# A two-layer f32 model on one core: values of two heads in one product, x and z two pairs ahead, and a residual round behind one more projection

## The chip, the cores and the metric

The kernel runs on one core of a Trainium2 chip. The metric is the device time of one execution in microseconds, taken as the median of several executions. The profile is of one further execution of the same program.

## The reference, cut to what matters

The model has two layers, each with a feed-forward block behind it, on 512 tokens of width 1024. The first layer, the one that the change touches, joins an SSD mixer (16 heads of width 64, in two groups that share B and C) and a gated linear attention, GLA (4 heads, keys of 128, values of 256):

```python
proj = h @ w_in
z, xbc, dt_raw, q, k, v, g, gk_low = jnp.split(proj, ...)
xbc = silu(causal_depthwise_conv(xbc, conv_w, conv_b))      # x, B, C
dt  = softplus(dt_raw + dt_bias);  a_cum = cumsum(dt * -exp(a_log))
cb  = einsum(cm, bm)                                        # per chunk of 128
y_diag = einsum(cb, decay, x * dt)
states = einsum(bm, to_end, x * dt)                         # carried over the chunks
y_off  = einsum(cm, prev, exp(a_cum))
y = rms_norm_by_group((y_diag + y_off + x * d_skip) * silu(z))
# GLA: gk = log_sigmoid(gk_low @ gk_w2 + gk_b) / 16, scores and states in chunks of 64, times v
x = x + concatenate([y_ssd, y_gla]) @ w_out
x = x + swiglu(rms_norm(x))
```

The second layer is multi-head latent attention (MLA), followed by another feed-forward block. All of it is in f32.

## The kernel before, in words

**Products.** Activations lie transposed: eight tiles of 128 features by 512 tokens. TensorE (PE) multiplies in the type fp32r, so each f32 operand is split into a high part (ScalarE, ACT, casts it) and a low part (VectorE, DVE, subtracts). A product of two such operands is three matmuls, hi·hi, lo·hi and hi·lo (`mm3`, L172 to L174); eight such triples give one 128x512 tile (`dense`). A weight tile goes from a DMA on SyncE's queue into `wraw` (two buffers), then into `whi` on ACT (L164) and `wlo` on DVE (L165), three buffers each. These weights are issued with a priority that puts them ahead of what stands near them in the program. A buffer is free again when the last matmul that reads it is done.

**Banks.** Large products take turns on three PSUM banks called `acc`. Further banks are used by name: `st` for small sums, `a1`, `a2` (two) and `xt`.

**Start.** PE first runs eight matmuls on zeros (L101). The input x arrives tile by tile, is split, and the first product (`dtgk`: time steps and the gate's low-rank input) follows it. The second product is B of the first group. The sum of squares gives R, the reciprocal norm of each token, which scales every product when it is read from its bank.

**Pairs.** The 16 SSD heads are worked as eight pairs. For each pair f there is x (`conv`: product, scale by R, four taps L422 and L425, a tanh gate), z (`z_gate`, L293 to L297), and then:

- `core_in`: a DMA spreads the cumulated decays over partitions (`acb`); ACT makes the decay matrix `mt` (L476, L478), which DVE multiplies by cb (L480); PE turns x token-major (L488); DVE makes `xdt` (L492) and `xde` (L496).
- `core_states`: three matmuls (L505), then `hs`: one ACT copy (L509) and four DVE steps (L512) that carry the state.
- `core_out`: outputs from states (L525, made to wait for the last step of `hs`), outputs from within the chunk (L533), and four DVE steps to `y` (L537 to L540).

PE's waits for these small steps are hidden by large products put between them: each group of small matmuls is ordered behind a chosen matmul of a large product. `finish` squares y, and behind the pairs 3 and 7 a group norm over four y (L207 to L224, L547) gives the parts (`mxh`, `mxl`, L140 and L141) of four tiles of the mixer's output.

Before, x and z of pair 2 were made between pair 0's inputs and outputs, the values of GLA's head 0 covered pair 1, and from there x and z of pair f+1 covered pair f. The values' products (`values`, one head at a time) were 128x256.

**Behind the pairs.** `values(2)` and `values(3)` stand behind pair 7. Then GLA starts: the small weight `gk_w2` is split into `gw` (L639 to L642) and multiplied (L648). `project(h)` makes q and k of a head from two large products (DVE reads them from their banks as `qd`, L679, and `kr`). `out_round(r)` multiplies four tiles of mixer output by w_out and adds the result to x; round 0 covers pair 7, round 1 stands behind `project(0)`, and `project(1)` behind that.

The order of each engine's instructions comes from a scheduler that walks the program with priorities; `order(i, j)` adds that i stands behind j.

Of the kernel before, what the change touches and what calls it, by code (L numbers as in the profile page):

```python
# [8 lines left out]
F32 = mybir.dt.float32  # L9
# [9 lines left out]
P = 128  # L19
# [27 lines left out]
def kernel(ctx: ExitStack, tc: tile.TileContext, A, yT, stop=99):  # L47
# [52 lines left out]
    for j in range(8):  # L100
        E.matmul(ps, idle[:, 0:P], idle, start=True, stop=True)  # L101
# [42 lines left out]
    hold = []  # L144
# [6 lines left out]
    def weight_now(src, kc, m, home):  # L151
        raw = wp.tile([P, KD * P], F32, tag="wraw", name=nm("wraw"), bufs=2)
        r = raw[:, :kc * m]
        nc.sync.dma_start(r.rearrange("p (k m) -> p k m", k=kc), src)
        return parts(r, kc, m, home)

    def parts(r, kc, m, home=None):
# [6 lines left out]
        S.copy(hi[:, :kc * m], r)  # L164
        i = V.tensor_tensor(lo[:, :kc * m], r, hi.bitcast(F32)[:, :kc * m], ALU.subtract)  # L165
        if hold:
            order(i, hold[0], "weights that can wait behind a chain that cannot")
        return (hi[:, :kc * m].rearrange("p (k m) -> p k m", k=kc),
# [58 lines left out]
    def rstd_log(ssq, n, pool, tag):  # L227
# [10 lines left out]
        S.activation(R, R, AF.Exp, scale=-0.5)  # L238
# [7 lines left out]
    class Norm:  # L246
# [18 lines left out]
        def square(self, c, behind=None, pool=res, bufs=2):  # L265
# [5 lines left out]
            if self.ssq is None:  # L271
                self.ssq = sq
            else:
                V.tensor_tensor(sq, self.ssq, sq, ALU.add)
                self.ssq = sq
# [14 lines left out]
    def gate(pool, tag, ps, R, bufs):  # L290

        h = pool.tile([P, T], F32, tag="cva", name=nm(tag + "h"), bufs=2)
        V.scalar_tensor_tensor(h, ps, 0.5, R, ALU.mult, ALU.mult)  # L293
# [10 lines left out]
    for c in range(KD):  # L304
        nrm.add(c, later=True)
    with tc.tile_pool(name="sq0", bufs=4) as sq0:
        for c in range(KD):
            nrm.square(c, nrm.last, sq0, 4)
# [26 lines left out]
    with tc.tile_pool(name="gkp", bufs=1) as gkp:  # L335

        ps = aux("a1")
        dense(ps[:48], w_dtgk, xp)
# [13 lines left out]
        def steps(behind):  # L352
# [28 lines left out]
            S.activation(av, alog, AF.Exp)  # L381
# [24 lines left out]
        with tc.tile_pool(name="ssd", bufs=2) as sp:  # L406
# [4 lines left out]
            mm, zmm = {}, {"states": []}  # L411

            def conv(i, tag, bufs, bank=acc):

                w = weight(A["w_xbc"][i], KD, P)
# [6 lines left out]
                S.activation(a, xpad[:, 3:], AF.Identity, bias=cw[:, 48 + i:49 + i],  # L422
                             scale=cw[:, 36 + i:37 + i])
                for k in range(3):
                    V.scalar_tensor_tensor(a, xpad[:, k:k + T], cw[:, 12 * k + i:12 * k + i + 1], a,  # L425
                                           ALU.mult, ALU.add)
# [29 lines left out]
            def z_gate(f):  # L456
# [3 lines left out]
                return gate(sp, "z", ps, R, 2)  # L460

            def core_in(f, xs, cb, behind=None):

                acb = sp.tile([P, 2, T], F32, tag="acb", name=nm("acb"))
# [4 lines left out]
                S.activation(te, te, AF.Exp)  # L469
                cd = sp.tile([P, 2, 2], F32, tag="cd", name=nm("cd"))  # L470
                S.activation(cd, last[:, 1:3, :], AF.Exp)

                mt = sp.tile([P, 2, 4, P], F32, tag="mt", name=nm("mt"))
                for h in range(2):
                    for c in range(4):
                        S.activation(mt[:, h, c, :], acb[:, h, c * P:(c + 1) * P], AF.Relu, scale=-1.0,  # L476
                                     bias=act[:, c, 2 * f + h:2 * f + h + 1])
# [5 lines left out]
                for h in range(2):  # L483
                    S.activation(ea[64 * h:64 * h + 64, :], acb[64 * h:64 * h + 64, h, P:], AF.Exp)

                ps = aux("xt")
                for c in range(4):
                    i = E.transpose(ps[:, c * P:(c + 1) * P], xs[:, c * P:(c + 1) * P], ident)  # L488
                    if behind is not None:
                        order(i, behind, "x token-major in one go with the outputs of the heads before")  # L490
                xdt = sp.tile([P, 4, 2, 64], F32, tag="xdt", name=nm("xdt"))
# [6 lines left out]
                return f, xs, mt, ea, cd, xdt, xde  # L498

            def core_states(part, btok, behind):  # L500

                f, xs, mt, ea, cd, xdt, xde = part
                pst = aux("a2")
                for c in range(3):
                    i = E.matmul(pst[:, c * P:(c + 1) * P], btok[:, c, :],  # L505
                                 xde[:, c].rearrange("p h e -> p (h e)"), start=True, stop=True)
                    order(i, behind, "states behind products that run until x is ready")
                hs = sp.tile([P, 3, P], F32, tag="hs", name=nm("hs"), bufs=1)
                S.copy(hs[:, 0, :], pst[:, 0:P])  # L509
# [7 lines left out]
                return hs, ready  # L517

            def core_out(part, state, zg, cT, behind):

                hs, ready = state
                f, xs, mt, ea, cd, xdt, xde = part
                po = aux("a2")
                for c in range(3):
                    i = E.matmul(po[:, c * P:(c + 1) * P], hs[:, c, :], cT[:, (c + 1) * P:(c + 2) * P],  # L525
                                 start=True, stop=True)
                    order(i, behind, "outputs behind products that run until the states are ready")
                    wait_for(i, ready, "outputs in one go")
# [24 lines left out]
            def values(h):  # L553

                mms = []
                wv = [weight(A["w_v"][h, j], 4, 256) for j in range(2)]
                v = gkp.tile([P, 4, 256], F32, name=f"v{h}")
                for i in range(4):
                    ps = acc()
                    for k in range(KD):  # L560
                        wh, wl = wv[k // 4]
                        xh, xl = xp[k]
                        mms.append(mm3(ps[:, :256], xh[:, i * P:(i + 1) * P], xl[:, i * P:(i + 1) * P],
                                       wh[:, k % 4, :], wl[:, k % 4, :], k == 0, k == KD - 1))
                    S.activation(v[:, i, :], ps[:, :256], AF.Copy, scale=rtok[:, i:i + 1])
                vt[h] = v
                return mms

            rounds, ys, sums_sq = [], [], []

# [32 lines left out]
            part = core_in(2, xs[2], cb, end)  # L603
# [766 lines left out]
```

## Time and profile before

| | |
|---|---|
| median of three runs | 1343.99 us (1343.94 to 1344.37) |
| the profiled execution | 1347.43 us |
| its span, first to last instruction | 1345.2 us |
| busy in the span: PE / DVE / ACT | 1333.2 / 813.8 / 566.4 us |
| matmuls of PE | 6506 |
| mean granted clock of PE | 0.997 |
| first layer's mixer, by PE's timeline | about 0 to 408 us |

The profile names a group of instructions by its line in the kernel, the engine, the operation, and what it writes from what. "Idle before" is the time for which the engine stood still ahead of an instruction, and the name behind the arrow is the instruction that the profile takes for the releaser. Matmuls overlap, so a matmul's own duration is longer than the step from one start to the next. The granted clock is the share of full speed at which PE was let run in that stretch.

### The profile page before, as it was taken

The page shows a single profiled execution, that of the slowest core. Times are in us where ns is not written, and L with a number is a line of the kernel's source. Part 1 is how long each engine was busy: PE and PEld are TensorE (multiplying, and loading weights), DVE is VectorE, ACT ScalarE, POOL GpSimd, SP SyncE. Part 2 cuts the span into 40 slices and gives each one's busy share as a digit, 9 for nine tenths or more (in the row PEclk, how much of TensorE's full clock was granted, in tenths as well). Part 3 has the DMA queues.
Part 4 walks back from the last instruction along what each step waited for, and adds up shares of the span by engine and source line. Part 5 has one row for each costly group of instructions (what it writes and reads, how often), then busy time and mean ns, then how long its engine had stood idle before and what let it go on. Part 6 is the DMA issues. An engine that isn't in the chain of part 4 may idle for free.

```text
span 1345.2 us, 16692 instructions
## 1 busy us (share of the span) xinstructions
PE 1333.2 (99%) x6506; PEld 1094.7 (81%) x6506; DVE 813.8 (60%) x1387; ACT 566.4 (42%) x958; POOL 7.8 (1%) x35
## 2 busy tenths in 40 slices
PE   9999999999999999999999999999999999999998
PEld 6788889888888888888888887777788888888887
DVE  7878977778977444444333368987674444443221
ACT  7575634534344222233223338986543322222111
POOL 0000000000000000000000000000000000000000
PEclk9999999999999999999999999999999999999999
DMA  5333232322233323333333321100123323333331
GB/s 180 127 110 111 79 94 82 95 64 78 70 103 94 95 94 101 103 94 95 93 91 102 100 78 56 66 32 32 56 92 104 95 94 95 100 103 94 114 107 62
DMA packets 36782, 122.23 MB, mean 91 GB/s; under 512 B 4768, under 2 KB 5792, under 8 KB 36704
## 3 DMA queue, kind: packets, MB, share of 16 engines
q1 hardware_dynamic: 35888, 120.72, 28.8%
q8 instruction: 51, 0.84, 0.3%
q10 hardware_dynamic: 816, 0.46, 0.1%
q14 instruction: 27, 0.22, 0.1%
HBM read 119.03 MB, written 2.13 MB: 90 GB/s over the span
## 4 chain that ended last, share of the span: by engine, by line
PE 88%; DVE 5%; ACT 4%; DMA 1%; issue 1%; POOL 0%; SPq 0%; ACTq 0%; POOLq 0%; DVEq 0%
PE acc L172 26%; PE acc L173 26%; PE acc L174 26%; PE sco L1114 2%; PE po L1161 1%; PE ptr L1142 1%; DVE wlo L165 1%; ACT whi L164 1%; PE a L533 1%; ACT mt L476 1%; PE a L757 1%; DVE cva L425 0%; PE a L525 0%; PE a L762 0%; ACT xh L259 0%
## 5 line engine op out<-in xcount | busy, mean ns | idle before, releaser
L164 ACT CAST whi<-wraw 128x1024 fp32r<-128x1024 f32 (+1 forms) x218 | 224.7, 1031 | 558.6 <-PE acc L173 421.3
L172 PE MATMUL acc<-xh,whi 128*128 128x512 f32 x1144 | 449.7, 393 | 0.2 <-ACT qT L1089 0.2
L173 PE MATMUL acc<-xl,whi 128*128 128x512 f32 x1144 | 446.0, 390 | 0.0
L174 PE MATMUL acc<-xh,wlo 128*128 128x512 f32 x1144 | 445.8, 390 | 0.0
L165 DVE TENSOR_TENSOR wlo<-wraw,whi 128x1024 fp32r<-128x1024 f32 (+1 forms) x218 | 260.6, 1195 | 150.2 <-ACT whi L164 149.7
L172 PEld LDWEIGHTS acc<-xh,whi 128*128 128x128 f32 x1144 | 214.9, 188 | 45.2 <-issue 0.8
L174 PEld LDWEIGHTS acc<-xh,wlo 128*128 128x128 f32 x1144 | 214.8, 188 | 44.7
L173 PEld LDWEIGHTS acc<-xl,whi 128*128 128x128 f32 x1144 | 214.9, 188 | 44.1 <-issue 0.4
L827 DVE TENSOR_TENSOR fu<-acc,R 128x512 f32<-128x512 f32 x44 | 30.4, 691 | 137.6 <-PE acc L174 137.6
L174 PE MATMUL acc<-fhh,wlo 128*128 128x512 f32 x288 | 112.0, 389 | 0.0
L172 PE MATMUL acc<-fhh,whi 128*128 128x512 f32 x288 | 112.0, 389 | 0.0
L173 PE MATMUL acc<-fhl,whi 128*128 128x512 f32 x288 | 112.0, 389 | 0.0
L824 DVE TENSOR_TENSOR fg<-acc,R 128x512 f32<-128x512 f32 x44 | 30.4, 691 | 89.3 <-PE acc L174 89.3
L172 PEld LDWEIGHTS acc<-fhh,whi 128*128 128x128 f32 x288 | 54.1, 188 | 11.3
L174 PEld LDWEIGHTS acc<-fhh,wlo 128*128 128x128 f32 x288 | 54.1, 188 | 11.2
L173 PEld LDWEIGHTS acc<-fhl,whi 128*128 128x128 f32 x288 | 54.1, 188 | 11.2
L172 PE MATMUL acc<-mxh,whi 128*128 128x512 f32 x128 | 49.9, 392 | 0.0
L173 PE MATMUL acc<-mxl,whi 128*128 128x512 f32 x128 | 49.7, 389 | 0.0
L174 PE MATMUL acc<-mxh,wlo 128*128 128x512 f32 x128 | 49.7, 389 | 0.0
L1127 ACT ACTIVATE sc<-sc,mx 128x128 f32<-128x128 f32 (+3 forms) x64 | 35.9, 565 | 12.3 <-DVE mx L1125 12.1
L1114 PE MATMUL sco<-kT,qT 96*128 96x256 f32 (+3 forms) x128 | 39.5, 440 | 0.8 <-ACT qT L1089 0.5
L841 DVE TENSOR_TENSOR x<-x,acc 128x512 f32<-128x512 f32 x16 | 11.0, 688 | 42.9 <-PE acc L174 42.9
(363 smaller groups left out, 1608.2 us busy)
## 6 DMA issues: line engine op xcount, KB each, us to landing
wraw<-in_w_gate_dram SPq DMA_DIRECT2D x44, 512.0 KB, 3.5
wraw<-in_w_up_dram SPq DMA_DIRECT2D x44, 512.0 KB, 3.5
wraw<-in_w_down_dram SPq DMA_DIRECT2D x32, 512.0 KB, 3.5
wraw<-in_w_out_dram SPq DMA_DIRECT2D x16, 512.0 KB, 3.5
wraw<-in_w_xbc_dram SPq DMA_DIRECT2D x12, 512.0 KB, 3.6
wraw<-in_w_down_dram SPq DMA_DIRECT2D x16, 384.0 KB, 3.1
wraw<-in_w_z_dram SPq DMA_DIRECT2D x8, 512.0 KB, 3.6
wraw<-in_w_v_dram SPq DMA_DIRECT2D x8, 512.0 KB, 3.6
```

Of the source, the lines that this page charges most:

```text
L164: S.copy(hi[:, :kc * m], r)
L165: i = V.tensor_tensor(lo[:, :kc * m], r, hi.bitcast(F32)[:, :kc * m], ALU.subtract)
L172: E.matmul(out, ah, bh, start=first, stop=False)
L173: E.matmul(out, ah, bl, start=False, stop=False)
L174: return E.matmul(out, al, bh, start=False, stop=last)
L476: S.activation(mt[:, h, c, :], acb[:, h, c * P:(c + 1) * P], AF.Relu, scale=-1.0, bias=act[:, c, 2 * f + h:2 * f + h + 1])
L533: i = E.matmul(pd[64 * h:64 * h + 64, c * P:(c + 1) * P], xdt[:, c, h, :], mt[:, h, c, :], start=True, stop=True)
L757: i = E.matmul(po[e][:, r * P:(r + 1) * P], v[:, r, e * P:(e + 1) * P], sc[:, r, :], start=True, stop=(r == 0))
L824: V.tensor_tensor(g, pg, R, ALU.mult)
L827: V.tensor_tensor(u, pu, R, ALU.mult)
L1114: i = E.matmul(ps[:, at:at + n], self.qts[j][:, b * P:(b + 1) * P], self.kts[j][:, :n], start=True, stop=True)
L1127: S.activation(sc[:, at:at + n], sc[:, at:at + n], AF.Exp, bias=mx[:, j:j + 1], scale=-1.0, accum_out=sm[:, j:j + 1])
```

## The change

In the order of the program:

1. **Start.** Ten matmuls on zeros instead of eight. The first product takes each triple in the order hi·xh, lo·xh, hi·xl. The second product's weights are loaded and split in two halves, ahead of the squares, and the other weights' DMAs are ordered behind them. One exponential (`av`) is put behind the one of R.
2. **Values.** `values(h)` makes heads h and h+1 side by side as 128x512 products on four banks, with eight halves of weights loaded per tile pair. `values(0)` stands behind pair 3, `values(2)` covers pair 7.
3. **Pairs.** Before pair 1's states stand x and z of pair 3, and so on: x and z are made two pairs ahead (z has three buffers). `out_round(0)` covers pair 6. New orders put the rest of a covering product behind the states, and decays, first taps and z halves behind the states ahead of them.
4. **Residual round.** `project(1)` stands ahead of `out_round(1)`.
5. **Smaller.** The copies into `gw` have a high priority. Weights with a `home` (MLA's) are loaded through a tile of their own (`wrb`) and not through `wraw`.

```diff
-    for j in range(8):
+    for j in range(10):
         E.matmul(ps, idle[:, 0:P], idle, start=True, stop=True)
...
-        raw = wp.tile([P, KD * P], F32, tag="wraw", name=nm("wraw"), bufs=2)
+        if home is None:
+            raw = wp.tile([P, KD * P], F32, tag="wraw", name=nm("wraw"), bufs=2)
+        else:
+            raw = const.tile([P, T], F32, tag="rsb", name=nm("wrb"))
...
+    raw = wp.tile([P, KD * P], F32, tag="wraw", name="wraw_b", bufs=2)
+    w_b = [wp.tile([P, KD * P], F32R, tag=t, name=t + "_b") for t in ("whi", "wlo")]
+    b_split = []
+    for j in range(2):
+        at = slice(j * T, j * T + T)
+        first_in.append(nc.sync.dma_start(raw[:, at].rearrange("p (k m) -> p k m", k=4),
+                                          A["w_xbc"][8][:, 4 * j:4 * j + 4]))
+        b_split.append((S.copy(w_b[0][:, at], raw[:, at]),
+                        V.tensor_tensor(w_b[1][:, at], raw[:, at], w_b[0].bitcast(F32)[:, at], ALU.subtract)))
...
-        dense(ps[:48], w_dtgk, xp)
+        for k, (xh, xl) in enumerate(xp):
+
+            E.matmul(ps[:48], w_dtgk[0][:, k, :], xh, start=(k == 0), stop=False)
+            E.matmul(ps[:48], w_dtgk[1][:, k, :], xh, start=False, stop=False)
+            E.matmul(ps[:48], w_dtgk[0][:, k, :], xl, start=False, stop=(k == KD - 1))
...
-            S.activation(av, alog, AF.Exp)
+            order(S.activation(av, alog, AF.Exp), rstd_log.last, "one change of table for both")
...
-                return gate(sp, "z", ps, R, 2)
+                z = gate(sp, "z", ps, R, 3)
...
-                wv = [weight(A["w_v"][h, j], 4, 256) for j in range(2)]
-                v = gkp.tile([P, 4, 256], F32, name=f"v{h}")
+                vt[h], vt[h + 1] = (gkp.tile([P, 4, 256], F32, name=f"v{h + e}") for e in range(2))
+                banks = [acc() for _ in range(3)] + [aux("a1")]
+                for q in range(4):
+                    raw = wp.tile([P, KD * P], F32, tag="wraw", name=nm("wraw"), bufs=2)
+                    with tc.high_priority(offset=AHEAD):
+                        for e in range(2):
+                            nc.sync.dma_start(raw.rearrange("p (k e m) -> p k e m", k=2, e=2)[:, :, e, :],
+                                              A["w_v"][h + e, q // 2, :, 2 * (q % 2):2 * (q % 2) + 2])
+                        wh, wl = parts(raw, 2, T)
+                    for i in range(4):
+                        for k in range(2):
+                            xh, xl = xp[2 * q + k]
+                            mms.append(mm3(banks[i], xh[:, i * P:(i + 1) * P], xl[:, i * P:(i + 1) * P],
+                                           wh[:, k, :], wl[:, k, :], (q, k) == (0, 0), (q, k) == (3, 1)))
...
-            hs = core_states(part, btok, zmm[2][3])
-            y, end = core_out(part, hs, zg[0], cT, zmm[2][7])
-            part = core_in(1, xs[1], cb, end)
+            hs = core_states(part, btok, zmm[2][1])
+
+            order(zmm[2][3], hs[3], "the rest of the product behind the states")
+            for i in (part[7][-2], part[7][-1], conv_ops["in", 2]):
+                order(i, hs[2], "what can wait behind the states")
+            for i in (conv_ops[2], z_ops[2]):
+                order(i, hs[1], "the next pair's behind the states")
+            y, end = core_out(part, hs, zg[0], cT, zmm[2][-1])
+            outs = list(out_ops)
+            part = core_in(1, xs[1], cb, end, hs[2])
             finish(0, y)
-            rtok = tok_scalar(R)
-            v = values(0)
-            hs = core_states(part, btok, v[5])
-            y, end = core_out(part, hs, zg[1], cT, v[27])
...
+            for f in range(1, 8):
...
+                if f < 6:
+                    xs[f + 2] = conv(f + 2, "xs", 3)
+                    fill = mm[f + 2]
+                elif f == 6:
+                    fill = out_round(0, rounds[0])
                 else:
-                    mms = out_round(0, rounds[0])
-                    hs = core_states(part, btok, mms[3])
-                    last = mms[11]
+                    fill = values(2)
...
             q0, _ = project(0)
+            q1, last = project(1)
             out_round(1, rounds[1])
-            q1, last = project(1)
```

**What it moves on the engines, first place: DVE between the first pair's outputs and the second pair's states.** The rows are DVE's list before, from the carried states of pair 0 (`hs_112`) to the operand of pair 1's states (`xde_123`). `cva` and `xs` belong to x, `zh` and `z` to z, `y_115` to pair 0's output.

```order
L512 SCALAR_TENSOR_TENSOR hs_112_665<-hs_112_665,cd_90_555,a2_111_661 128x64 x4
L480 TENSOR_TENSOR mt_119_696<-mt_119_696,cb_76_489 128x512 x2
L538 TENSOR_TENSOR ea_92_569<-a2_113_671,ea_92_569 128x384
L165 TENSOR_TENSOR wlo_153_911<-wraw_151_908,whi_152_910 128x1024
L537 SCALAR_TENSOR_TENSOR y_115_684<-xs_58_375,pv_87,a2_114_675 128x512
L492 TENSOR_TENSOR xdt_122_716<-xt_121_711,dt_398 128x512
L539 TENSOR_TENSOR y_115_684<-y_115_684,ea_92_569 128x384
L496 TENSOR_TENSOR xde_123_718<-xdt_122_716,te_117_691 128x384
```

After the change the same stretch of DVE's list ends in these rows. Ahead of them, behind the four steps of pair 0's `hs`, stand two `cva` taps, `zh` and a third `cva` tap.

```order
L499 TENSOR_TENSOR te_143_837<-acb_142_835,act_553 128x6
L576 TENSOR_TENSOR ea_89_574<-a2_110_676,ea_89_574 128x384
L458 SCALAR_TENSOR_TENSOR xs_100_627<-cvt_99_625,cva_98_620 128x512
L307 SCALAR_TENSOR_TENSOR z_107_664<-zt_106_662,zh_105_660 128x512
L575 SCALAR_TENSOR_TENSOR y_112_689<-xs_55_380,pv_87,a2_111_680 128x512
L511 TENSOR_TENSOR mt_116_701<-mt_116_701,cb_73_494 128x512
L577 TENSOR_TENSOR y_112_689<-y_112_689,ea_89_574 128x384
L511 TENSOR_TENSOR mt_116_701<-mt_116_701,cb_73_494 128x512
L578 TENSOR_TENSOR y_112_689<-y_112_689,z_63_444 128x512
L527 TENSOR_TENSOR xdt_119_721<-xt_118_716,dt_403 128x512
L171 TENSOR_TENSOR wlo_153_872<-wraw_151_869,whi_152_871 128x1024
L531 TENSOR_TENSOR xde_120_723<-xdt_119_721,te_114_696 128x384
```

So `xde` of pair 1 now has the taps, z and x of pair 2 and all of y ahead of it, where before it had `mt`, two steps of y and a weight split. On PE, the states that read it stand 26 large matmuls behind the transposes (L522).

**Second place: PE at the second head's projections.** The rows are PE's list after the change, from the last triple of q1 into k1. `acc_412` is q1's bank, `acc_419` k1's; three banks back, `acc_395` is q0's. The names in brackets are engines for which the instruction waits.

```order
L180 MATMUL acc_412_2264<-xh_19_157,whi_410_2260 128x512
L181 MATMUL acc_412_2264<-xl_20_158,whi_410_2260 128x512
L182 MATMUL acc_412_2264<-xh_19_157,wlo_411_2261 128x512
L180 MATMUL acc_419_2303<-xh_5_129,whi_417_2299 128x512 [waits DVE_49,Activation_49]
L181 MATMUL acc_419_2303<-xl_6_130,whi_417_2299 128x512
L182 MATMUL acc_419_2303<-xh_5_129,wlo_418_2300 128x512
L709 MATMUL st_387_2145<-gx_245,gw_2132 128x512 [waits DMAHW3_49,DMAHW4_49,DMAHW1_49,DMAHW5_49,DMAHW0_49,DMAHW6_49,DVE_49,Activation_49]
```

Before, residual round 1 stood here, and the first product behind the values was q0, 24 matmuls later k0.

**Third place: DVE ahead of that matmul.** DVE's list after the change, from the last scalings of the group norm to the reads of the banks of q0, k0 and q1. `mxl` are the low parts of the mixer's output, `wlo_432` the low parts of residual round 1's second weights.

```order
L585 SCALAR_TENSOR_TENSOR y_342_1878<-y_342_1878,pv_87,Rg_378_2094 128x512
L141 TENSOR_TENSOR mxl_380_2107<-y_279_1539,mxh_379_2106 128x512
L141 TENSOR_TENSOR mxl_382_2112<-y_308_1680,mxh_381_2111 128x512
L141 TENSOR_TENSOR mxl_384_2117<-y_342_1878,mxh_383_2116 128x512
L585 SCALAR_TENSOR_TENSOR y_372_2078<-y_372_2078,pv_87,Rg_378_2094 128x512
L171 TENSOR_TENSOR wlo_432_2378<-wraw_430_2375,whi_431_2377 128x1024
L141 TENSOR_TENSOR mxl_386_2122<-y_372_2078,mxh_385_2121 128x512
L740 SCALAR_TENSOR_TENSOR qd_397_2204<-acc_395_2177,R_32_203 128x512
L753 TENSOR_TENSOR kr_403_2241<-acc_402_2216,R_32_203 128x512
```

Before, DVE's list at the reads of q0 and k0 was this:

```order
L650 TENSOR_SCALAR gm_2331<-st_398_2332,pv_87 128x512
L650 TENSOR_SCALAR gm_2331<-st_399_2336,pv_87 128x512
L679 SCALAR_TENSOR_TENSOR qd_408_2391<-acc_406_2364,R_32_192 128x512
L165 TENSOR_TENSOR wlo_426_2478<-wraw_424_2475,whi_425_2477 128x1024
L650 TENSOR_SCALAR gm_2331<-st_400_2340,pv_87 128x512
L650 TENSOR_SCALAR gm_2331<-st_401_2344,pv_87 128x512
L692 TENSOR_TENSOR kr_414_2428<-acc_413_2403,R_32_192 128x512
```

The weight parts rotate over three buffers (`wlo` in the order q0, k0, q1, k1, then the round's first and second weights), so `wlo_432` takes the buffer that q1's `wlo_411` held.

More of the change, by code (lines that the diff above doesn't have):

```diff
@@ L167, in parts @@
             order(i, hold[0], "weights that can wait behind a chain that cannot")
+        if len(hold) > 1:
+            order(cast, hold[1], "weights that can wait behind a chain that cannot")
         return (hi[:, :kc * m].rearrange("p (k m) -> p k m", k=kc),
@@ L273, in square @@
             else:
-                V.tensor_tensor(sq, self.ssq, sq, ALU.add)
+                i = V.tensor_tensor(sq, self.ssq, sq, ALU.add)
+                if behind_sum is not None:
+                    order(i, behind_sum, "sums of squares behind the first weights")
                 self.ssq = sq
@@ L483, in core_in @@
                 for h in range(2):
-                    S.activation(ea[64 * h:64 * h + 64, :], acb[64 * h:64 * h + 64, h, P:], AF.Exp)
+                    act_ops.append(S.activation(ea[64 * h:64 * h + 64, :], acb[64 * h:64 * h + 64, h, P:], AF.Exp))
+                if behind_act is not None:
+                    for i in act_ops:
+                        order(i, behind_act, "decays behind the states of the heads before")
                 ps = aux("xt")
@@ L516, in core_states @@
                                                ALU.mult, ALU.add)
-                return hs, ready
+                return hs, ready, first, last
             def core_out(part, state, zg, cT, behind):
-                hs, ready = state
-                f, xs, mt, ea, cd, xdt, xde = part
+                hs, ready = state[:2]
+                f, xs, mt, ea, cd, xdt, xde = part[:7]
                 po = aux("a2")
+                out_ops.clear()
                 for c in range(3):
@@ new lines @@
+            for f in range(1, 8):
+                cT_out = cT
+                if f == 3:
+                    bc = group(1)
+                if f < 6:
[3 more added lines that the diff above has]
+                    fill = out_round(0, rounds[0])
+                else:
+                    fill = values(2)
+                if f == 1:
+                    for i in outs:
+                        order(i, fill[1], "first outputs behind products that run until the decays are ready")
+                    order(fill[3], part[8], "the rest of the products behind x token-major")
+                hs = core_states(part, btok, fill[5 if f == 1 else 4])
+                if f == 3:
+                    cb, cT, btok = spread(*bc, fill[-1])
+                if f < 6:
+                    zg[f + 2] = z_gate(f + 2)
+                    last = zmm[f + 2][-1]
+                else:
+                    order(fill[6], hs[3], "the rest of the products behind the states")
+                    last = fill[11]
@@ L622 @@
                     part = core_in(f + 1, xs[f + 1], cb, end)
+                if f > 5:
+                    order(fill[13], part[8] if f < 7 else end, "the rest of the products behind the outputs")
                 finish(f, y)
-                if f in (3, 7):
-                    values(1 if f == 3 else 2)
-            values(3)
+                if f == 3:
+                    rtok = tok_scalar(R)
+                    values(0)
         with tc.tile_pool(name="gla", bufs=2) as gp:
```

85 lines of the change are left out of this document (41 added, 44 removed).

## The prediction

> **What bounds the kernel now.** I read the page's head first, then the windows of the stretches where the granted clock is not full, then the timeline around them.
>
> ```profile
> span 1345.2 us, 16692 instructions
> PE 1333.2 (99%) x6506; PEld 1094.7 (81%) x6506; DVE 813.8 (60%) x1387; ACT 566.4 (42%) x958; POOL 7.8 (1%) x35
> ```
>
> PE is busy for 99% of the span. So the kernel gets shorter only where PE issues less, where PE waits, or where its clock is low. The windows (span of each, PE, PEld, DVE, ACT, POOL busy, granted clock, DMA share, GB/s) show the two places of low clock, each behind a slice in which PE was partly idle:
>
> ```profile
> 4.02:7.44 3.42, 2.11 (x8) 0.49 (x6) 2.20 (x4) 2.45 (x5) 0.00 (x0) 1.00 1.01 359
> 7.44:10.85 3.41, 3.41 (x9) 1.58 (x10) 3.41 (x6) 3.41 (x6) 0.00 (x0) 0.50 1.04 414
> 65.46:68.88 3.42, 0.46 (x4) 0.44 (x4) 3.23 (x9) 3.40 (x8) 0.10 (x1) 1.00 0.30 117
> 68.88:72.29 3.41, 3.41 (x25) 2.85 (x24) 3.14 (x5) 1.92 (x7) 0.00 (x0) 0.50 0.41 154
> ```
>
> The second is the only long wait of PE. In PE's timeline (start, duration) the first two rows are the first pair's outputs; the other two bracket the same three groups (L525, L533, L488) of a later pair at full clock:
>
> ```profile
> 68.47 1.25 PE L525 MATMUL a<-cT,hs 128*128 128x128 f32 x6 [2.96 <-ACT mt L478]
> 72.31 0.36 PE L173 MATMUL acc<-wlo,xh 128*128 128x256 f32 x1
> ...
> 85.50 0.83 PE L525 MATMUL a<-cT,hs 128*128 128x128 f32 x6
> 87.70 0.48 PE L174 MATMUL acc<-xh,wlo 128*128 128x512 f32 x1
> ```
>
> The wait is 2.96 us. The three groups then take 72.31 − 68.47 = 3.84 us against 87.70 − 85.50 = 2.20, so the low clock costs 1.64 more: 4.6 us together. The row names ACT's exponential, but DVE's hs rows (below, 67.47 to 68.33) end just as PE starts, and the outputs are made to wait for hs.
>
> **Part 1, values side by side.** Matmuls overlap, so I price them from start to start: 25 steps between the first two rows, 36 between the last two.
>
> ```profile
> L172 PE MATMUL acc<-whi,xh 128*128 128x256 f32 x128 | 36.5, 285 | 0.0
> ...
> 223.76 0.28 PE L173 MATMUL acc<-wlo,xh 128*128 128x256 f32 x1
> 226.76 0.28 PE L174 MATMUL acc<-whi,xl 128*128 128x256 f32 x1
> ...
> 399.62 0.39 PE L172 MATMUL acc<-mxh,whi 128*128 128x512 f32 x1
> 407.78 0.39 PE L172 MATMUL acc<-xh,whi 128*128 128x512 f32 x1
> ```
>
> A 128x256 step is 3.00 / 25 = 0.120 us, a 128x512 step 8.16 / 36 = 0.2267. Each of the three lines of a triple has 128 narrow ones: 384 × 0.120 = 46.1 becomes 192 × 0.2267 = 43.5. **−2.6 us.** The same bytes come in twice as many, smaller DMAs, and evictions remain 32 halves; both lie under products.
>
> **Part 2, the start.** PE's second product, and what DVE and ACT do before it:
>
> ```profile
> 13.57 0.40 PE L172 MATMUL a<-xh,whi 128*128 128x512 f32 x1
> ...
> 6.55 4.75 DVE L260 SCALAR_TENSOR_TENSOR xl<-x,pv,xh 128x512 fp32r<-128x512 f32 x7 [0.68 <-ACT xh L259]
> ...
> 11.46 1.04 ACT L164 CAST whi<-wraw 128x1024 fp32r<-128x1024 f32 x1
> ...
> 12.54 1.23 DVE L165 TENSOR_TENSOR wlo<-wraw,whi 128x1024 fp32r<-128x1024 f32 x1 [0.25 <-ACT whi L164]
> ```
>
> The last xl ends at 11.30. At full clock the first product could end some three steps later, about 12.0, and the halved casts, ahead of the squares, would have the second product's weights by then: 13.57 − 12.0 = 1.6, at most 1.9. If the slice from 7.44 runs at half clock again, PE still has nearly the same 24 matmuls to do, and only the new order of each triple and the split casts help: 0.4. Two more idle matmuls raise the busy share of the slice at 4.02, where 2.11 of 3.42 was not enough. Between 0.4 and 1.9 I take **−1.2**.
>
> **Part 3, pairs 0 and 1.** The next pair's x and z products now stand where 128x256 products stood, so hs is reached in time, and the wait with its clock slice goes: **−4.6**. But DVE runs its list in order, and what is late next is the second pair's states. From the end of hs DVE has (order in the section on the change) three conv taps, the z half, then ea, xs, z, y, the two mt, two more steps of y, xdt, a weight split, and xde. Their prices:
>
> ```profile
> 63.70 1.53 DVE L425 SCALAR_TENSOR_TENSOR cva<-xpad,cw,cva 128x512 f32<-128x512 f32 x2
> ...
> 65.94 0.68 DVE L293 SCALAR_TENSOR_TENSOR zh<-acc,R 128x512 f32<-128x512 f32 x1
> ...
> 67.47 0.86 DVE L512 SCALAR_TENSOR_TENSOR hs<-hs,cd,a 128x64 f32<-128x64 f32 x4
> 68.43 1.29 DVE L480 TENSOR_TENSOR mt<-mt,cb 128x512 f32<-128x512 f32 x2
> ...
> 70.24 1.22 DVE L165 TENSOR_TENSOR wlo<-wraw,whi 128x1024 fp32r<-128x1024 f32 x1
> 71.68 0.75 DVE L537 SCALAR_TENSOR_TENSOR y<-xs,pv,a 128x512 f32<-128x512 f32 x1 [0.22 <-PE a L533]
> 72.59 0.69 DVE L492 TENSOR_TENSOR xdt<-xt,dt 128x512 f32<-128x512 f32 x1 [0.16 <-PE xt L488]
> 73.20 0.55 DVE L539 TENSOR_TENSOR y<-y,ea 128x384 f32<-128x384 f32 x1
> 73.66 0.55 DVE L496 TENSOR_TENSOR xde<-xdt,te 128x384 f32<-128x384 f32 x1
> 74.13 0.69 DVE L540 TENSOR_TENSOR y<-y,z 128x512 f32<-128x512 f32 x1
> ```
>
> With ea as the L539 row and xs and z as the L540 row: 1.53 + 0.77 + 0.68 + 0.55 + 0.69 + 0.69 + 0.75 + 1.29 + 0.55 + 0.69 + 0.69 + 1.22 + 0.55 = 10.65; successive rows start about 0.09 before the one ahead ends (73.20 + 0.55 against 73.66), twelve times: 9.6. PE over the same stretch has the three groups, 2.20, and 26 products, 5.9: 8.1. So the second states wait **+1.5** (0.5 to 2). The first states are asked for two triples earlier (6 × 0.2267 = 1.36; nothing shows their slack): +0.5 (0 to 1.4). The second outputs: +0.3 (0 to 1.5). Sum +2.3, and if such a wait falls into one clock slice, up to 1.64 more, which I keep for the range.
>
> **Part 4, the residual round later.** This is the counter-cost. PE now runs the products q0, k0, q1, k1 in a row on three banks, so the first matmul of k1 waits until DVE's qd has read q0's bank. In DVE's list qd stands behind the last split of the norm (mxl) and behind a weight split (wlo_432) whose buffer is free only when q1's last matmul is done: pools of weights have three buffers. That is a fixed chain. Its rows before, DVE's, and ACT's cast:
>
> ```profile
> 205.78 0.75 DVE L537 SCALAR_TENSOR_TENSOR y<-xs,pv,a 128x512 f32<-128x512 f32 x1 [0.48 <-PE a L533]
> ...
> 225.56 0.69 DVE L141 TENSOR_TENSOR mxl<-y,mxh 128x512 fp32r<-128x512 f32 x1 [0.69 <-ACT mxh L140]
> 226.78 1.22 DVE L165 TENSOR_TENSOR wlo<-wraw,whi 128x1024 fp32r<-128x1024 f32 x1 [0.53 <-ACT whi L164]
> 227.92 0.67 DVE L640 TENSOR_TENSOR gw<-w,wt 16x512 fp32r<-16x512 f32 x1
> ...
> 234.22 0.68 DVE L679 SCALAR_TENSOR_TENSOR qd<-acc,R 128x512 f32<-128x512 f32 x1
> ...
> 225.69 1.05 ACT L164 CAST whi<-wraw 128x1024 fp32r<-128x1024 f32 x1 [0.17 <-PE acc L174]
> ```
>
> From the start of q1's last matmul: its 0.39; a hand-over 0.14 (hs ends 68.33, PE starts 68.47); cast to split 226.78 − 225.69 = 1.09; split to next 227.92 − 226.78 = 1.14; mxl 0.60 (0.69 less the overlap); qd 0.68; a hand-over 0.14: 4.18. The next step would have come at 0.23, so k1 loses 3.95. DVE may be later than that: from the last outputs its norm took 226.25 − 205.78 = 20.5 with two weight splits; four more (4 × 1.14), of which its idle there hides some, make 22 to 25 us to mxl's end, against 87 products × 0.2267 + 0.39 + 0.14 + 1.09 + 1.14 + 0.60 = 23.0 by the chain. So 4 to 6; I take **+4.2**. Before, 20 us of value products covered all of this.
>
> Would the clock fall behind it? The slice of 65.46 was followed by half clock with 0.46 us busy, and that of 4.02 with 2.11 busy. A 4 us idle leaves some slice with 2 us of work or less, so by these rows it falls: **+1.6** (0 to 3.2, if two slices fall). [...]
>
> **Part 5, the rest.** These waits of before bear on the gw copies and on MLA's weights, which now load through a tile of their own:
>
> ```profile
> PE st L648 <- ACT gw L642: 0.4, 1, 0.4
> ...
> PE sco L1114 <- ACT qT L1089: 0.5, 1, 0.5
> PE acc L1086 <- ACT v L1008: 0.4, 1, 0.4
> PE sco L920 <- DVE lsq L908: 0.4, 1, 0.4
> ```
>
> The gw copy still ends behind qd, so 0.4 stays. Earlier weights in MLA may take the 0.4 of lsq and some of the other two: **−0.5** (−1.3 to +0.5).
>
> **Sum.** −2.6 − 1.2 − 4.6 + 2.3 + 4.2 + 1.6 − 0.5 = −0.8 us. The profiled execution took 1347.43 us (span 1345.2, 2.2 around it), so it would take 1346.6. Its own time is 3.4 above the median of the runs shown, 1343.99 (1343.94 to 1344.37); the same sum on that median gives **1343.2**. About 0.2%, 2.7 us, is what a measurement of this kernel can tell from no change.
>
> **Rivals.** *The k1 chain is covered* (chance 0.2). If something I read in the order releases qd earlier, the +4.2 and +1.6 go: −6.6, 1337.4. For it: DVE is busy only 60% overall. Against it: the list is in order and the buffer is one of three. *The gains hold and the clock does not fall* (0.15): −2.6 − 1.6 − 4.6 + 1.5 + 4 − 0.5 = −3.8, 1340.2; against it stands the slice at 4.02. [...] *Slower by the clock* (0.17): the waits of 1.5 at the second states and of 4 to 6 at k1 each drop the clock for a slice, k1's for two, and the start keeps its half-clock slice. Then −2.6 − 0.4 − 4.6 + 2.3 + 1.6 + 5 + 3.2 − 0.5 = +4.0, 1348.0. It decides from the point at which the new waits and their slices exceed the 8.4 us that parts 1, 2 and 3 give back.
>
> **How the numbers follow.** My forecast, the gains eaten at k1, has 0.48; within it the bounds of start and states move the sum from −2.7 to +2.5. The first two rivals are faster by over 0.2% (0.35), the third is slower (0.17). The range from 1338.0 to 1347.6 leaves out about half of the first rival and half of the third.
>
> **What would show it.** Right: PE idle of about 4 us just before the fourth product behind the last values, released by DVE's qd, with a slice at 0.5 clock behind it; no wait at the first outputs, a wait of 1 to 2 us at the second pair's states; narrow matmuls gone. Wrong: no gap ahead of k1, or a full clock behind one; a second product that still starts after 13 us; new waits elsewhere in the pairs.

## The result, and the profile after

The changed kernel takes 1349.44 us (median of six runs, 1347.88 to 1349.85) against 1344.03 for before (1343.82 to 1344.44). The ratio is 1.0036, with a 95% interval of 1.0026 to 1.0046: slower by 5.4 us, clear of 0.2%, and above the range of the prediction. The profiled execution of the changed kernel took 1349.53 us, so its trace stands for its usual runs.

The page's head, and behind it the largest of PE's waits over the whole span that the trace of before does not have in this size (total, times, longest):

```profile
span 1347.3 us, 16322 instructions
PE 1332.4 (99%) x6316; PEld 1084.3 (80%) x6316; DVE 812.3 (60%) x1388; ACT 562.2 (42%) x957; POOL 7.8 (1%) x35
```

```profile
PE acc L180 <- DVE qd L740: 4.1, 1, 4.1
PE a L540 <- DVE xde L531: 1.4, 1, 1.4
...
PE a L823 <- ACT st L810: 0.8, 1, 0.8
PE st L709 <- ACT gw L703: 0.7, 1, 0.7
```

The two largest new waits are the two that the order showed: k1 behind DVE's read of q0's bank, and pair 1's states behind `xde`. The wait at pair 0's outputs is gone. PE's timeline at k1, and the windows of that stretch, laid so that one begins where the clock falls and one where it comes back (the granted clock is the third number from the end):

```profile
236.05 0.39 PE L182 MATMUL acc<-xh,wlo 128*128 128x512 f32 x1
240.55 0.47 PE L180 MATMUL acc<-xh,whi 128*128 128x512 f32 x1 [4.11 <-DVE qd L740]
...
242.20 0.79 PE L709 MATMUL st<-gx,gw 80*128 80x512 f32 x1 [0.71 <-ACT gw L703]
242.79 0.63 PE L180 MATMUL acc<-xh,whi 128*128 128x512 f32 x1
...
248.34 0.49 PE L180 MATMUL acc<-xh,whi 128*128 128x512 f32 x1
```

```profile
238.30:241.72 3.42, 0.94 (x3) 0.49 (x3) 3.38 (x6) 1.10 (x3) 1.85 (x5) 1.00 0.42 122
241.72:245.13 3.41, 2.93 (x7) 2.31 (x8) 1.22 (x2) 1.11 (x2) 0.10 (x1) 0.50 0.08 31
245.13:248.54 3.41, 3.41 (x9) 2.64 (x9) 0.75 (x1) 0.69 (x1) 0.00 (x0) 0.50 0.00 0
248.54:251.95 3.41, 3.41 (x16) 2.72 (x16) 1.62 (x3) 1.95 (x3) 0.00 (x0) 1.00 0.00 0
```

k1 loses 240.55 − 236.05 − 0.23 = 4.27 us. Then 13 steps from 242.79 to 248.34 take 5.55 where 2.95 would do, and with the gate's matmul ahead of them (0.59 for 0.23) the clock costs some 3.0: two slices at half, not one. All six runs of the changed kernel have the mean granted clock of this trace, 0.997.

The trace of before on which the prediction was made was not of a usual run: it took 1347.43 us, 3.4 above the median. The first experiment below gave a usual one (1344.00 us, span 1341.8), and the account is made against that. Between it and the trace after, the span grows by 5.5:

| stretch | us |
|---|---|
| start, to the first product on `acc` | −1.96 |
| values side by side, by their steps | −2.6 |
| pairs 0 and 1: wait of 1.38 at states for one of 0.92 at outputs | +0.5 |
| k1's wait | +4.3 |
| half clock behind it | +3.0 |
| gate's wait, 0.71 for 0.42 | +0.3 |
| GLA's first score to the feed-forward block | +1.7 |
| sum | +5.2 |

The first and the last line come from these rows, of the usual run of before and then of after: the first product on `acc`, the first score, and the first product of the first feed-forward block's second half.

```profile
25.87 0.39 PE L172 MATMUL acc<-xh,whi 128*128 128x512 f32 x1
...
269.33 0.27 PE L718 MATMUL a<-qd,ki 128*64 128x64 f32 x1
644.77 0.39 PE L172 MATMUL acc<-fhh,whi 128*128 128x512 f32 x1
```

```profile
23.91 0.40 PE L180 MATMUL acc<-xh,whi 128*128 128x512 f32 x1
...
272.82 0.27 PE L779 MATMUL a<-qd,ki 128*64 128x64 f32 x1
649.97 0.39 PE L180 MATMUL acc<-fhh,whi 128*128 128x512 f32 x1
```

From score to feed-forward it is 375.44 before and 377.15 after.

### The profile page after: what moved, and what is told of

It reads as the page before. It is cut to its first block, busy times and chain, and to the rows that moved or that the text cites. A ratio compares the mean times of both kernels' runs of the same rounds, so it can differ in the third digit from the quotient of the medians.

```text
span 1347.3 us, 16322 instructions
## 1 busy us (share of the span) xinstructions
PE 1332.4 (99%) x6316; PEld 1084.3 (80%) x6316; DVE 812.3 (60%) x1388; ACT 562.2 (42%) x957; POOL 7.8 (1%) x35
## 4 chain that ended last, share of the span: by engine, by line
PE 85%; DVE 8%; ACT 3%; DMA 2%; issue 2%; POOL 0%; SPq 0%; DVEq 0%; ACTq 0%; POOLq 0%
PE acc L180 25%; PE acc L181 25%; PE acc L182 25%; PE sco L1175 2%; DVE wlo L171 2%; PE ptr L1203 1%; PE po L1222 1%; DMA acb<-acd 1%; PE a L571 0%; PE a L818 0%; DVE cva L452 0%; ACT whi L170 0%; PE a L823 0%; DVE st L1084 0%; ACT xh L267 0%
## 5 line engine op out<-in xcount | busy, mean ns | idle before, releaser
L170 ACT CAST whi<-wraw 128x1024 fp32r<-128x1024 f32 (+2 forms) x217 | 223.4, 1029 | 560.9 <-PE acc L181 408.3
L171 DVE TENSOR_TENSOR wlo<-wraw,whi 128x1024 fp32r<-128x1024 f32 (+2 forms) x217 | 259.2, 1194 | 143.6 <-ACT whi L170 143.1
```

The costliest lines, as they stand in the source:

```text
L170: cast = S.copy(hi[:, :kc * m], r)
```

## The experiments

Every ratio below is to runs of the kernel before on the same chip (medians 1343.7 to 1343.9), with its 95% interval. The changed kernel was measured beside a median of 1344.0, so a difference to it, or between two experiments, is uncertain by some 0.3 us for that alone.

**1. Before, once more.** No edit.

> The kernel before, once more. Theory: the profiled execution of before (1347.43 us) fell 3.4 us above its median because its two half-clock slices (start, and behind the 2.96 us wait, about 1.5 and 1.64 us) are not in its usual runs; then this profile shows at most one of them and a time near 1344.0. Rival: both slices are always there and something else makes up the 3.4; then the profile shows both again, with a span near 1345.2.

Measured: 1344.00 us, ratio 1.0004 (0.9996 to 1.0013). The profile has full clock from 9.4 us on (PE's steps are 0.43 us until then and 0.23 behind it). Its first outputs, the slice of 3.4 us in which they wait, and the slice behind it:

```profile
67.08 0.91 PE L525 MATMUL a<-cT,hs 128*128 128x128 f32 x6 [0.92 <-ACT mt L478]
```

```profile
64.00:67.40 3.40, 2.48 (x22) 2.31 (x21) 3.21 (x9) 3.38 (x8) 0.10 (x1) 1.00 0.34 135
67.40:70.80 3.40, 3.40 (x38) 3.11 (x37) 3.40 (x6) 3.14 (x10) 0.00 (x0) 1.00 0.43 154
```

The wait is 0.92 us, not 2.96, and the clock holds. SyncE's queue shows why. It issues the store of the decays (`acd`) and, when that has landed, the load that spreads them (`acb`): first the trace behind the prediction, then the usual run.

```profile
48.76 0.34 SPq L396 DMA_DIRECT2D acd<-acf  x1
52.97 0.82 SPq L465 DMA_DIRECT2D acb<-acd  x2
```

```profile
49.30 0.34 SPq L396 DMA_DIRECT2D acd<-acf  x1
51.10 1.82 SPq L465 DMA_DIRECT2D acb<-acd  x2
```

The load starts 4.2 us behind the store in the one, where the store takes 4.2 from issue to landing, and 1.8 in the other. DVE and ACT wait for what it brings, DVE for 2.37 us in the one and 0.47 in the other:

```profile
56.87 0.17 DVE L468 TENSOR_TENSOR te<-acb,act 128x6 f32<-128x6 f32 x1 [2.37 <-DMA acb<-acd]
```

```profile
55.51 0.17 DVE L468 TENSOR_TENSOR te<-acb,act 128x6 f32<-128x6 f32 x1 [0.47 <-DMA acb<-acd]
```

So 2 us of that wait, and the half clock behind it, belonged to that execution, and such executions are rare: of 96 further runs of before (the 11 of this experiment and the 85 that the ratios below are taken to), one took over 1347 us, and it alone has that trace's mean clock of 0.997. The start differs less: it is partly at half clock in both traces, so the expectation was right only on the second slice. Why the store takes longer in some executions is not shown.

**2. k1 in another bank.** The changed kernel with

```diff
                 w = weight(A["w_k"][h], KD, P)
-                ps = acc()
+                ps = aux("a1") if h == 1 else acc()
```

> The changed kernel, with k1 in the bank a1, so that its first matmul doesn't wait for DVE's read of q0's bank. Theory: the wait of 4.1 us and the half clock behind it (13 to 15 steps longer by 0.2, some 3 us) both go: 1349.4 - 7 = 1342.4, with the gw wait of 0.7 left. Rival: DVE's list is the bound, and the wait moves on to the gate's products (gw) or to the first output of the residual round: 1347 to 1350, with an idle of 3 us or more within 6 us behind the old place.

Measured: 1342.22 us, ratio 0.9988 (0.9979 to 0.9997). PE's longest waits from 13 to 300 us:

```profile
PE a L540 <- DVE xde L531: 1.3, 1, 1.3
PE xt L802 <- DVE sc L787: 0.9, 1, 0.9
PE st L709 <- ACT gw L703: 0.4, 1, 0.4
```

No wait at k1, full clock there (a mean of 0.998 to 1.000 in the eleven runs), −7.2 us: one bank held all of the loss, and more than all. DVE's list, unchanged, holds nothing else up by 3 us.

**3. Cover for the idle.** The changed kernel with matmuls of no use ahead of k1:

```diff
+                if h == 1:
+                    ps = aux("a1")
+                    for j in range(18):
+                        i = E.matmul(ps, xp[0][0][:, 0:P], xp[0][0], start=True, stop=True)
+                        order(i, mms[-1], "cover behind the queries")
                 w = weight(A["w_k"][h], KD, P)
...
+                if h == 1:
+                    order(ks[0], i, "keys behind the cover")
```

> The changed kernel, with 18 matmuls of no use (x's high part times itself, into the free bank a1; 18 x 0.2267 = 4.1 us) between q1 and k1, where PE was idle for 4.1 us. Theory: the wait itself stays, the clock doesn't fall: 1349.4 - 3 = 1346.4, granted clock 1.0 throughout there. Rival: the slices at half clock have another cause than the idle: no change, 1349.4.

Measured: 1344.78 us, ratio 1.0008 (0.9999 to 1.0017), 4.7 below the changed kernel. The windows show 1.00 in the slice behind k1's start:

```profile
238.80:242.20 3.40, 3.40 (x15) 2.36 (x13) 3.37 (x6) 1.08 (x3) 1.93 (x5) 1.00 0.40 131
242.20:245.60 3.40, 3.13 (x14) 2.42 (x14) 1.14 (x2) 1.43 (x3) 0.02 (x1) 1.00 0.06 23
```

k1 starts as late behind q1 as in the changed kernel, and the clock loss is gone. So the idle causes the half clock. The two traces differ by less than the medians, 3.8 us of span: some 3.0 is the clock, 0.4 a shorter gate's wait (0.3 for 0.7), 0.9 lies in GLA and behind it (376.3 us for 377.15 from the first score to the feed-forward block), and the start gives some of it back.

**4. The split behind the reads.** The changed kernel with one order more:

```diff
...
             w = weight(A["w_out"][r, m2], 4, 256)
+            if r == 1 and m2 == 1:
+                order(lows[-1], reads[0], "the round's second weights behind the queries")
```

> The changed kernel, with the split of the round's second weights (wlo_432, which waits for q1's last matmul through its buffer) put behind the reads of q0's and k0's banks on DVE. Theory of the prediction (the chain through the buffer is what holds qd): qd comes 1.14 us earlier at least, the wait falls from 4.1 to 3.0 or less: 1348.3 or less. Rival (the norm's own tail holds it: last y scaled, ACT's cast of it, DVE's low part, all late from DVE's list): qd comes only some 0.4 us earlier, wait 3.7, 1349.0.

Measured: 1348.65 us, ratio 1.0038 (1.0026 to 1.0051); k1 waits 3.9. DVE's list ahead of the read of q0's bank in this run:

```profile
239.95 0.75 DVE L588 SCALAR_TENSOR_TENSOR y<-y,pv,Rg 128x512 f32<-128x512 f32 x1
241.38 0.69 DVE L141 TENSOR_TENSOR mxl<-y,mxh 128x512 fp32r<-128x512 f32 x1 [0.68 <-ACT mxh L140]
242.11 0.69 DVE L743 SCALAR_TENSOR_TENSOR qd<-acc,R 128x512 f32<-128x512 f32 x1
```

The split is gone from there, and DVE stands idle for ACT's cast instead. This execution was the slowest of its five (1350.68 us), and the median lies between the two forecasts, so neither time decides. The rows do: from the end of the last `y` to the read it is 1.41 us here and 1.78 in the trace after (its rows stand below), 0.4 less, as the rival had it. So the norm's tail is late by itself. The buffer of `wlo_432` was a second holder of about the same length, not the holder.

**5. `xde` first.** Run 2's kernel with

```diff
...
             part = core_in(1, xs[1], cb, end, hs[2])
+            for i in (conv_ops["out", 2], z_ops["out", 2]):
+                order(i, core_in.xde, "the next pair's x and z behind this pair's states")
```

> The changed kernel with k1 in the bank a1 (1342.2 us), and pair 2's last steps of x and z put behind pair 1's xde on DVE. Theory: the second states wait 1.3 to 1.5 us because xde stands behind x, z and a weight split on DVE; those three go from ahead of it (0.69 + 0.69 + 1.22, less overlap, 2.3 us), so the wait goes: 1342.2 - 1.3 = 1340.9. Rival: the wait only moves to the outputs of pair 1 or to pair 2: 1342.2.

Measured: 1341.48 us, ratio 0.9980 (0.9971 to 0.9989). From 13 to 260 us PE has one wait left (GLA's `sc`, 0.8, comes behind that):

```profile
PE st L712 <- ACT gw L706: 0.5, 1, 0.5
```

The medians differ by 0.7, less than the 1.3 expected, with overlapping spreads. The states' wait is gone from this trace, but the traces of the other experiments do not bear out that the edit took it. The load of the decays stood closer behind its store in this execution, and the wait follows that:

| traces | load behind store | wait at pair 1's states |
|---|---|---|
| after, runs 2, 3, 4 and 11 | 3.9 to 4.3 us | 1.3 to 2.1 us |
| runs 6 and 7 | 2.6 us | 0.2 us and none |
| runs 5 and 10, `xde` first | 2.9 us | none |
| run 12, `xde` first | 4.1 us | 0.7 us |

Run 7 has the order of the changed kernel here and no wait. DVE needs as long from `hs` to `xde` in both (9.98 us in after, 9.90 in run 7), but in run 7 `hs` is done 1.6 us before PE starts the outputs, in after 0.4. By the one trace of run 12 the edit is worth some 0.6 us or more where the load is late; where it is early there was little to win.

**6. The round ahead again.** The changed kernel with

```diff
-            q1, last = project(1)
             out_round(1, rounds[1])
+            q1, last = project(1)
```

> The changed kernel with only its fourth part undone: the residual round ahead of project(1) again. Theory: what went missing is the 10 us of value products behind pair 7 that covered the group norm; PE then comes to the round 63 products (14.3 us) behind the last outputs, mxl is ready after some 21, so the k1 wait, its clock and the loss in the attention's scores (4.3 + 3.0 + 0.4 + 1.7) go and a wait of 5 to 7 us with one or two half-clock slices (1.6 to 3.2) comes at the round's first output: 1349.4 - 9.4 + 8.4 = 1348.4. Rival: the moved round is at fault alone; then no new wait: about 1340.

Measured: 1348.54 us, ratio 1.0037 (1.0024 to 1.0050). PE's waits from 100 to 300 us, and two slices:

```profile
PE acc L180 <- ACT mxh L140: 4.5, 1, 4.5
PE acc L181 <- DVE mxl L141: 0.5, 1, 0.5
```

```profile
233.80:237.20 3.40, 1.59 (x3) 0.98 (x4) 3.40 (x6) 1.86 (x3) 0.00 (x0) 0.53 0.56 154
237.20:240.60 3.40, 3.40 (x10) 2.63 (x9) 2.40 (x4) 0.62 (x1) 0.81 (x2) 0.50 0.00 0
```

So the late round is not the fault alone. With it undone a wait of the same length, for the norm's parts, stands at the round's first output. GLA's loss did not go with the k1 wait, as the theory had it: first score to feed-forward is 376.50 us, 1.1 more than in the usual run of before. The likely reason is that the norm lost its cover because values that stood behind pair 7 moved to pair 7; the second head's projection only takes the round's place as cover, and is stopped by the bank. No run puts the values back in the changed kernel, but run 8, which has wide values behind pair 7 in the kernel before, shows no such wait.

**7. Eight matmuls on zeros.** Run 2's kernel with

```diff
-    for j in range(10):
+    for j in range(8):
```

> The changed kernel with k1 in the bank a1 (1342.2 us), and eight matmuls on zeros at the start, not ten. Theory: the two more let the clock rise some 3.4 us earlier; without them the first product runs at half clock till 9 us, as in before, and the second starts some 1.3 us later: 1343.5. Rival: the order of the triples and the halved weights make the earlier start: 1342.2 or less.

Measured: 1342.16 us, ratio 0.9990 (0.9981 to 0.9999), the same as run 2. The rival holds: the two more do nothing that can be measured in the time.

**8. Values only.** The kernel before with the changed `values`, called for heads 0 and 2:

```diff
...
-                if f in (3, 7):
-                    values(1 if f == 3 else 2)
-            values(3)
+                if f == 7:
+                    values(2)
```

> The kernel before (1343.9 us), with the values of two heads side by side and nothing else: heads 0 and 1 where head 0 stood, heads 2 and 3 behind pair 7, none behind pair 3. Theory: 192 x 0.2267 in place of 384 x 0.120, -2.6 us: 1341.3. Rival: weights for 512 columns and the fourth bank bring waits that eat it, or the wider products are no cheaper: 1343.9.

Measured: 1343.15 us, ratio 0.9995 (0.9986 to 1.0004): no difference that can be told. Its trace has waits that the usual run of before has not, or shorter:

```profile
PE a L525 <- DVE te L468: 1.2, 1, 1.2
PE a L505 <- DVE xde L496: 1.2, 1, 1.2
PE xt L748 <- DVE sc L733: 0.8, 1, 0.8
```

The states of pair 5, at 159.76 us, now wait for `xde` (1.19), and the scores cost 1.2 more over the same stretch (376.62 us for 375.44). By the medians some 2 of the 2.6 us of the steps are given back. This trace shows where it can happen, but it is of the slowest of the eleven runs (1344.68 us), so that these waits stand in the usual run is not shown.

**9. The start only.** The kernel before with the changed start (triples' order, weights in halves, the moved exponential), eight matmuls on zeros:

> The kernel before (1343.8 us) with the start of the changed one alone: triples in the new order, second product's weights in halves ahead of the squares, one exponential moved; eight matmuls on zeros. Theory: the start is the one part that gives its full price, and gives it without the two more matmuls: PE's first product for a pair starts 1.4 to 2.5 us earlier (25.87 us in a usual run of before, 23.4 to 24.5 in the changed ones): 1342.0. Rival: the time gained comes back as a wait for R's chain or at the first pair: 1343.8.

```diff
...
-        dense(ps[:48], w_dtgk, xp)
+        for k, (xh, xl) in enumerate(xp):
+            E.matmul(ps[:48], w_dtgk[0][:, k, :], xh, start=(k == 0), stop=False)
+            E.matmul(ps[:48], w_dtgk[1][:, k, :], xh, start=False, stop=False)
+            E.matmul(ps[:48], w_dtgk[0][:, k, :], xl, start=False, stop=(k == KD - 1))
...
-                w = weight(A["w_xbc"][i], KD, P)
+                w = w_b if i == 8 else weight(A["w_xbc"][i], KD, P)
```

Measured: 1345.63 us, ratio 1.0005 (0.9996 to 1.0014), inconclusive. The twelve runs lie in two groups, five from 1342.1 to 1343.3 and seven from 1345.6 to 1347.3. The profiled one is of the first (1342.91 us), with the gain at the start (first product on `acc` at 24.73 us for 25.87), a wait of 0.8 at pair 0's outputs and full clock behind the start. The second group stands 3.6 us higher, about as far as the trace behind the prediction stood above its median. The clock parts the two groups: the mean granted clock is 1.000 in each of the five and 0.997 to 0.999 in each of the seven. What takes it down in the seven was not seen, since none of them was profiled.

**10. Gates later.** Run 5's kernel with

```diff
...
-            out_round(1, rounds[1])
+            order(gates[0], out_round(1, rounds[1])[3], "gates behind the round's first triples")
```

> The fifth run's kernel (k1 in bank a1, xde first; 1341.5 us), with the gate's products (gw times gx) behind the first triples of the residual round, not within k1. Theory: the gw wait of 0.5 goes and nothing takes its place: 1341.0. Rival: the gates are then late for the first scores, which wait as long: 1341.5 or more.

Measured: 1341.15 us, ratio 0.9975 (0.9965 to 0.9986). The gate's wait is gone; one of 0.5 at GLA's first scores, for DVE's `kr`, takes its place. Against run 5 nothing can be told. It is the fastest version here, 2.8 us below before.

**11. Half the cover.** Run 3's kernel with 8 matmuls, not 18.

> The changed kernel with 8 matmuls of no use between q1 and k1 where the third run had 18: PE is idle for 4.1 - 1.8 = 2.3 us. Theory of the prediction (a slice with two of its 3.4 us idle drops the clock in the next): half clock for one slice, 1.64 us above the third run's 1344.8: 1346.4. Rival one, only an almost wholly idle slice drops it: 1344.8, clock 1.0 throughout. Rival two, every long wait costs two slices: 1348.

Measured: 1346.37 us, ratio 1.0015 (1.0007 to 1.0024). The slice with the wait and the two behind it, in the profiled execution (1347.96 us, the slowest of eleven):

```profile
237.40:241.10 3.70, 1.67 (x8) 1.05 (x6) 3.67 (x6) 1.39 (x2) 0.27 (x1) 1.00 0.02 8
241.10:244.50 3.40, 3.00 (x7) 2.45 (x8) 2.04 (x4) 1.23 (x2) 1.67 (x5) 0.51 0.40 146
244.50:248.00 3.50, 3.50 (x16) 2.74 (x16) 1.13 (x2) 1.38 (x2) 0.00 (x0) 0.99 0.00 0
```

One slice at half clock behind 2.4 us of idle, and a median 1.6 us above run 3: the prediction's reading of the clock, not that of an almost wholly idle slice. By the runs' mean clocks it does not hold for every execution. Three of the eleven runs have a mean clock of 1.000 and took 1344.67 to 1345.26 us, as run 3; the other eight, at 0.998 to 0.999, took 1345.97 to 1347.96.

**12. Without MLA's tile.** Run 5's kernel with every weight through `wraw`:

```diff
-        if home is None:
-            raw = wp.tile([P, KD * P], F32, tag="wraw", name=nm("wraw"), bufs=2)
-        else:
-            raw = const.tile([P, T], F32, tag="rsb", name=nm("wrb"))
+        raw = wp.tile([P, KD * P], F32, tag="wraw", name=nm("wraw"), bufs=2)
```

> The fifth run's kernel (1341.5 us) without the tile of their own for MLA's weights with a home. The prediction credited that tile with 0.5 us: 1342.0 without it. Rival: it does nothing that can be measured: 1341.5, and the waits of PE in MLA are the same.

Measured: 1341.37 us, ratio 0.9980 (0.9972 to 0.9989). PE waits in MLA for `qT` (0.5), `v` (0.4) and `kT` (0.2), as in run 5, and from the feed-forward product above to the end of the span it is 697.4 us here and 697.6 in run 5. The tile does nothing that can be measured. This trace has a wait of 0.7 at pair 1's states again, with `xde` first (see run 5).

## Why the prediction was wrong, point by point

- **What failed: part 3's credit, −4.6.** The 2.96 us wait and its 1.64 of clock were rows of an execution that took 3.4 us more than the median. The prediction set the sum against both, saw the 3.4, and still carried the same credit to the median. Run 1 has 0.92 and no half clock there, so of 4.6 some 3.7 were not there to win. That turns the sum of −0.8 into +2.9. The rest to +5.4 is mainly the clock behind k1 (+1.4 over its forecast) and GLA (+1.7), less 0.8 that part 2 gave beyond its forecast and 0.9 by which part 3's new waits stayed below theirs.
- **Too small: the clock behind k1.** Forecast +1.6 with 3.2 as the end; after shows 3.0, two slices. Run 3 shows that the idle causes it, and run 11 that 2.4 us of it can be enough.
- **Not foreseen: GLA's +1.7.** Each kernel with the new values has 0.9 to 3.0 us more from the first score to the feed-forward block, at different waits (`st` in after, `sc` in runs 2 and 8). Run 8 shows it with the values alone. What in the order of DVE and ACT does it stays open; it was not tried.
- **Part 1: right price, little gain.** The steps are 2.6 shorter, and run 8's median is only 0.6 below before; its trace has waits that could take the rest back.
- **Part 2: right, and larger.** −1.96 for −1.2 in the trace. The reason given was half wrong: the two more matmuls on zeros do nothing that can be measured (run 7). Run 9 could not show the start's gain in the time.
- **Part 3's new wait: right for this trace, and in part luck.** 1.38 us idle for a forecast loss of 1.5; the +0.5 and +0.3 for the first states and second outputs did not show. The sum over DVE's list was sound, but the wait also hangs on when the decays' load lands, which the forecast left out: in run 7 the same list brings no wait (see run 5). DVE needed 72.34 − 62.36 = 9.98 us from the end of `hs` to the end of `xde` in the trace after, for the 9.6 that were added up from rows of before:

```profile
61.51 0.85 DVE L548 SCALAR_TENSOR_TENSOR hs<-hs,cd,a 128x64 f32<-128x64 f32 x4
...
71.79 0.55 DVE L531 TENSOR_TENSOR xde<-xdt,te 128x384 f32<-128x384 f32 x1
```

- **Part 4: the wait right, 4.27 for 4.2, its holder only half.** In the trace after, ACT's cast for the split and DVE's backlog end within 0.6 us of each other, and run 4 shows that the norm's tail alone holds `qd` as long:

```profile
236.30 1.05 ACT L170 CAST whi<-wraw 128x1024 fp32r<-128x1024 f32 x1 [0.16 <-PE acc L181]
...
237.19 0.74 DVE L585 SCALAR_TENSOR_TENSOR y<-y,pv,Rg 128x512 f32<-128x512 f32 x1
237.86 1.22 DVE L171 TENSOR_TENSOR wlo<-wraw,whi 128x1024 fp32r<-128x1024 f32 x1
238.99 0.68 DVE L141 TENSOR_TENSOR mxl<-y,mxh 128x512 fp32r<-128x512 f32 x1
239.71 0.69 DVE L740 SCALAR_TENSOR_TENSOR qd<-acc,R 128x512 f32<-128x512 f32 x1
```

- **Part 5.** The gate's wait grew by 0.3; MLA's tile gave nothing that can be measured for the −0.5 (run 12).
- **The rivals.** The third, slower by the clock at 1348.0, comes nearest, through its wait at k1 with two slices. Its price is near in part by luck: it too held part 3's credit, and against that it counted a half-clock start and a slice behind the states' wait, which the trace after does not show. The second, in which the clock does not fall, is not borne out: it fell to 0.50 behind 4.11 us of idle in after, and to 0.51 over the slice behind 2.44 us in run 11.

## What to carry to other kernels

A profile is one execution: when its own time is well above the median, look for what in it is not usual before crediting the removal of it. When cover moves, follow the chain that it covered to the next thing that waits on the same engine's list; here the group norm took some 4 us at k1 and at the round's first output alike, and a fourth bank for k1 cost nothing and gave it all back. A wait that is gone from one trace is not yet taken by the edit: see whether it is also gone without the edit in another execution, as the states' wait was here. A gain in matmul steps is a gain only where no small wait stands ready to take it.

## What the runs showed of the hardware that was not expected

- A 32 KB store to memory, followed by a load of the same data, let the load start 1.8 us behind the store in one execution and 4.2 in another, of the same program; over the fourteen traces here it is 1.8 to 4.3.
- The granted clock fell to 0.5 for one slice of 3.4 us behind idles of 2.44 (run 11), 2.96 (the trace behind the prediction) and 3.92 us (run 4), and for two behind idles of 4.11 (after) and 4.46 us (run 6). It held behind one of 0.92 (run 1). The slices that end where it falls hold 1.33, 0.46, 0.10, 0.94 and 0.10 us of PE's work, in this order, and the one at the start of before held 2.11 (the prediction's row at 4.02). None of the six is wholly idle.
- When it comes back is not explained by PE's busy time alone: it came back after one slice at half clock with 2.80 of 3.41 us busy (run 4) and 3.06 (run 11), and stayed at half for a second one after 2.93 (after) and 1.78 (run 6).
